# Feed-forward stages in plain record order, and squares kept apart for the ones product

## The chip, the cores and the metric

One core of a Trainium2 chip runs the whole program in one launch. The time is the device time of one execution in microseconds; three executions of the kernel before are shown, and one more was profiled. All data are fp32. TensorE (PE) multiplies, VectorE (DVE) and ScalarE (ACT) work elementwise out of and into on-chip memory, GpSimd (POOL) takes a few additions, and SyncE (SP) issues the loads.

## The reference

512 tokens of width 1024 go through a two-layer transformer and then through one more block. A layer is: half a feed-forward (`swiglu_ffn`), a mixer (banded attentions or recurrences), a cross-attention to a memory, and half a feed-forward again, each behind an RMS norm and added to its input. The last block is a recurrence with sparse attention, an RMS norm, and a feed-forward whose output is normed. Five feed-forwards in all, of width 2816. What the change touches is this:

```python
def rms_norm(x, g):
    y = x * lax.rsqrt(jnp.mean(x * x, axis=-1, keepdims=True) + RMS_EPS)
    return y * g

def swiglu_ffn(x, w_gu, w_down):
    gate, up = jnp.split(x @ w_gu, 2, axis=-1)
    return (jax.nn.silu(gate) * up) @ w_down
```

## The kernel before

The tokens' features lie on the partitions: eight blocks `X[b]` of 128 features by 512 tokens. A product in fp32 is made of three in a shorter type (`mm3`, lines 299 to 305): each factor is split into a high and a low part, hi·hi, hi·lo and lo·hi. Weights are loaded by SP (L296), their high part is cast on ACT (L297) and the low part subtracted on DVE (L298). The inputs of a norm's products are GH (L569, ACT) and GL (L570, DVE), the block times the norm's gain, split; the norm's factor, one per token, is multiplied onto the product's result.

The sum of squares that this factor needs is gathered block by block: ACT squares a block (L166), POOL adds it to `sqacc` (L168). Then a product with a column of ones (L534, in `rms_tokens`; eight matmul records for 512 tokens) sums over partitions, and four transposes (L547) spread the factor over them.

A feed-forward is a list of steps. Two plain groups of 48 matmuls of 512 columns (`plain(0)`, `plain(1)`, each two matrices over eight blocks kt) come first; the ones product is recorded behind the first, `rms.R` behind the second. In the last feed-forward `halves` stands in place of both, with the ones product behind it. Then come units (`unit`): seven products of 24 matmuls of 256 columns on sums and differences of quarters of weights, in place of eight products. Their weights are quarter tiles `fq` (six buffers) summed on DVE (L433, L437, L440, L444) and split on ACT (L416) and DVE (L417), four buffers each; `keep` copies a product's bank aside (L467, ACT), `out` adds it to another bank (L659, L661, DVE), and `act` makes the gate: Silu (L623, ACT), product (L624, DVE), split (L506 ACT, L507 DVE). Among the units stand the steps of the down product (`down`), whose result `add_half` adds to X (L755) and, for the last chunk, hands to `block_done`: GH, GL, square, and for a norm ahead of a feed-forward the sums of two blocks that the units need (`pair_done`, L387 to L392, split by L506 and L507).

The order is made by the tile scheduler: each recorded instruction has its place in the record as its priority, and on each engine the first of those that are ready goes first. `high_priority()` gives what is recorded in it the first place of all; with an offset it shifts the place by so many records. `run_steps` records the preparations (loads and splits) of a step three steps ahead, under `high_priority`. Weights (L296 to L298), GH and GL, the copies of `keep` and the additions of L659 have it too.

Below, A to E are the five feed-forwards in order of time: A 0 to 398 us, B from 831, C from 1184, D from 1999, E from 2887 to the end. Four of them (A, B, C, D) add to X by `add_half`, and each is followed by a mixer or by another stage that starts from X.

Of the kernel before, what the change touches and what calls it, by code (L numbers as in the profile page):

```python
# [18 lines left out]
S = 512  # L19
# [7 lines left out]
NEG = -1e30  # L27
WB = 4

ORDER = (0, 4, 1, 5, 2, 6, 3, 7)  # L30
# [124 lines left out]
class Squares:  # L155
# [4 lines left out]

    def add(self, x):
        first = not self.parts
        if first:
            self.parts.append(self.net.tp.tile([P, 512], F32, name=self.net.uid("sqacc"), tag="sqacc", bufs=1)[:, :])
        sq = self.parts[0] if first else self.net.scratch()
        self.net.nc.scalar.activation(sq, x, AF.Square)  # L166
        if not first:
            self.net.nc.gpsimd.tensor_add(self.parts[0], self.parts[0], sq)  # L168


class Net:
    def __init__(self, ctx, tc, a):
        self.ctx, self.tc, self.nc, self.a = ctx, tc, tc.nc, a
        pool = lambda name, bufs, **k: ctx.enter_context(tc.tile_pool(name=name, bufs=bufs, **k))
        self.cp = pool("const", 1)
        self.wp = pool("weights", 1)
        self.tp = pool("temps", 2)
        self.sp = pool("small", 4)
        self.ps = pool("psum", 8, space=bass.MemoryType.PSUM)
        self.room = ctx.enter_context(tc.tile_pool(name="slots", bufs=38, reuse_waits="tile"))  # L180
        self.live = self.peak = 0
        self.n = 0
        self.scope = None
        self.phase("mix")
        self.setup()
# [34 lines left out]
    def bank(self):  # L220
        t = self.ps.tile([P, 512], F32, name=self.uid("bank"), tag="bank")
        return t

    def small(self, n, tag, bufs=2):
# [62 lines left out]
    def weights(self, w, nk, c):  # L287

        nc = self.nc
        n = nk * c  # L290
        raw = self.wp.tile([P, 1024], F32, name=self.uid("raw"), tag="raw", bufs=2)
        hi = self.wp.tile([P, 1024], F32R, name=self.uid("whi"), tag="whi", bufs=WB)
        lo = self.wp.tile([P, 1024], F32R, name=self.uid("wlo"), tag="wlo", bufs=WB)
        v = lambda t: t[:, :n].rearrange("p (k c) -> p k c", k=nk)
        with self.tc.high_priority():
            nc.sync.dma_start(raw[:, :n], w.block(nk, c))  # L296
            nc.scalar.copy(hi[:, :n], raw[:, :n])  # L297
            nc.vector.tensor_sub(lo[:, :n], raw[:, :n], hi[:, :n].bitcast(F32))  # L298
        return v(hi), v(lo)
# [49 lines left out]

    def feat_group(self, W, order=None):  # L350

        ps = [self.bank() for _ in W]
        order = order or ORDER
        for kt in order:
            for (wh, wl), p in zip(W, ps):
                self.mm3(p, wh[:, kt, :], wl[:, kt, :], self.GH[kt], self.GL[kt], kt == order[0], kt == order[-1])
        return ps
# [62 lines left out]
    def unit(self, load, B, done):  # L420
# [42 lines left out]
        def keep(b, name):  # L463
            def go():
                s = kept[name] = self.get()
                with self.tc.high_priority():
                    nc.scalar.copy(s.f, banks[b])  # L467
            return go
# [19 lines left out]
    def run_steps(self, steps, ahead=3):  # L488

        n = 0  # L490
        for i, (_, go) in enumerate(steps):
            while n < min(len(steps), i + 1 + ahead):
                if steps[n][0]:
                    with self.tc.high_priority():
                        steps[n][0]()
                n += 1
            go()


# [62 lines left out]

    def block_done(self, b, c=slice(0, S)):

        nc = self.nc
        gname, layer = self.gain
        g = self.col(gname, layer * ND + b)
        with self.tc.high_priority():
            nc.scalar.mul(self.GH[b][:, c], self.X[b][:, c], g)  # L569
            nc.vector.scalar_tensor_tensor(self.GL[b][:, c], self.X[b][:, c], g, self.GH[b][:, c].bitcast(F32), OP.mult, OP.subtract)  # L570
        if c.stop == S:
            self.sq.add(self.X[b])
            self.there.add(b)
            if self.pairs is not None and (b + 4) % ND in self.there:
                self.pair_done(b % 4)
# [35 lines left out]
    def ffn(self, nxt, wg, wu, wd, resid, tail=None, also=None):  # L611
# [9 lines left out]
        def act(f, t):  # L621
            g, u = t[:, 0, :], t[:, 1, :]
            nc.scalar.activation(g, g, AF.Silu)  # L623
            nc.vector.tensor_mul(u, u, g)  # L624
            hh, hl = self.get(2)
            self.split(hh.r, hl.r, u)
            HH[f], HL[f] = hh, hl
# [7 lines left out]
        def up(f):  # L635
# [11 lines left out]
            def done(which, bank, slot):  # L647
# [6 lines left out]
                if which == "21":  # L654
                    nc.vector.tensor_mul(o, v(bank), R(c))
                    act(f + 1, T[1])
                    return
                with self.tc.high_priority():
                    nc.vector.tensor_add(o, v(bank), v(slot))  # L659
                if which == "12":  # L660
# [34 lines left out]
        def plain(z):  # L695
            p.extend(self.feat_group(W[z], range(ND) if first else None))
            if z == 0:
                rms.y
            else:
                start()  # L700
# [926 lines left out]
    def out_norm(self, w, XH, XL, gname):  # L1627
# [30 lines left out]
        def update(z, R):  # L1658
            c = half[z]
            for b in ORDER:  # L1660
                m = mix[b].f[:, c]
                (nc.gpsimd if b % 2 else nc.vector).tensor_mul(m, m, R)
                nc.vector.scalar_tensor_tensor(self.X[b][:, c], m, self.col(gname, b), self.X[b][:, c], OP.mult, OP.add)  # L1663
                self.block_done(b, c)

# [364 lines left out]
```

## Time and profile before

| | us |
|---|---|
| three executions | 3302.57, 3307.66, 3314.03 |
| their median | 3307.66 |
| the profiled execution | 3308.28 |
| its span on the core | 3306.5 |
| TensorE busy in it | 3185.9 (96%) |
| VectorE busy | 2254.3 (68%) |
| ScalarE busy | 1609.7 (49%) |
| GpSimd busy | 392.8 (12%) |

The rows below are of the profiled execution. Times in a timeline count from the start of the span. A busy time of two overlapping matmuls counts once. "[12.89 <-POOL sqacc L168]" behind a row means that the engine had stood idle for 12.89 us and that an instruction of POOL on line 168 released it. PEclk 1.00 is the full TensorE clock of 2.4 GHz, 0.50 is 1.2 GHz.

### The profile page before, as it was taken

The numbers are of one execution on the slowest core, as the hardware profiler recorded it, in microseconds if no ns is written. First come the engines' busy times: TensorE is split into PE (matmuls) and PEld (weight loads), VectorE is DVE, ScalarE is ACT, GpSimd is POOL, SyncE is SP. The second block draws the span as 40 slices with busy tenths as digits, with TensorE's granted clock in tenths as the row PEclk, the third lists the DMA queues.
The fourth block names the chain that finished last, engine by engine and source line by source line (L and its number), as shares of the span: only waits on it lengthen the run. The fifth ranks groups of instructions, "written<-read, shape, count | busy, mean of one in ns | idle before, by whom it ended". The sixth has DMA issues, their size and how long they took to land. (4 is left out here: it accounts for less than half of the span.)

```text
span 3306.5 us, 51122 instructions
## 1 busy us (share of the span) xinstructions
PE 3185.9 (96%) x20508; PEld 2864.2 (87%) x20508; DVE 2254.3 (68%) x3384; ACT 1609.7 (49%) x2684; POOL 392.8 (12%) x606
## 2 busy tenths in 40 slices
PE   6999999999999989999999999999999999979998
PEld 5999888898899979998998988999877888769987
DVE  7877656656777688775566557776679455477765
ACT  4544445555444354444455554443486266344434
POOL 1000122201000010001122010000322132220001
PEclk8999998999999999999999999999999999989999
DMA  3333211332233223322223322332322322413331
GB/s 121 116 104 94 82 52 55 106 109 83 79 98 106 90 86 106 104 90 82 90 74 107 120 78 74 106 102 74 103 64 93 106 65 71 153 39 103 102 90 64
DMA packets 104334, 300.81 MB, mean 91 GB/s; under 512 B 13856, under 2 KB 17440, under 8 KB 104096
## 3 DMA queue, kind: packets, MB, share of 16 engines
q1 hardware_dynamic: 94464, 287.74, 27.1%
q10 hardware_dynamic: 9632, 9.80, 1.1%
q8 instruction: 160, 2.62, 0.3%
q14 instruction: 78, 0.64, 0.1%
HBM read 291.21 MB, written 6.29 MB: 90 GB/s over the span
## 5 line engine op out<-in xcount | busy, mean ns | idle before, releaser
L303 PE MATMUL bank<-slot,whi 128*128 128x256 f32 (+1 forms) x2768 | 913.8, 331 | 20.3 <-ACT slot L467 12.2
L304 PE MATMUL bank<-slot,whi 128*128 128x256 f32 (+1 forms) x2768 | 912.2, 330 | 0.2 <-DVE slot L507 0.2
L305 PE MATMUL bank<-slot,wlo 128*128 128x256 f32 (+1 forms) x2768 | 911.8, 330 | 0.0
L416 ACT CAST whi<-fq 128x1024 fp32r<-128x1024 f32 x350 | 365.9, 1048 | 550.3 <-PE bank L304 470.0
L297 ACT CAST whi<-raw 128x1024 fp32r<-128x1024 f32 (+3 forms) x363 | 345.5, 953 | 509.0 <-PE bank L304 286.1
L303 PEld LDWEIGHTS bank<-slot,whi 128*128 128x128 f32 x2768 | 522.6, 189 | 77.8 <-ACT slot L467 16.4
L304 PEld LDWEIGHTS bank<-slot,whi 128*128 128x128 f32 x2768 | 523.0, 189 | 54.5 <-DVE slot L507 3.3
L305 PEld LDWEIGHTS bank<-slot,wlo 128*128 128x128 f32 x2768 | 524.3, 189 | 50.8
L303 PE MATMUL bank<-gh,whi 128*128 128x256 f32 (+1 forms) x1712 | 542.9, 318 | 26.1 <-ACT whi L416 9.2
L298 DVE TENSOR_TENSOR wlo<-raw,whi 128x1024 fp32r<-128x1024 f32 (+3 forms) x363 | 406.7, 1121 | 219.7 <-ACT whi L297 218.3
L304 PE MATMUL bank<-gl,whi 128*128 128x256 f32 (+1 forms) x1712 | 540.6, 316 | 10.1 <-DVE gl L570 9.8
L417 DVE TENSOR_TENSOR wlo<-fq,whi 128x1024 fp32r<-128x1024 f32 x350 | 427.3, 1223 | 174.9 <-ACT whi L416 174.5
L305 PE MATMUL bank<-gh,wlo 128*128 128x256 f32 (+1 forms) x1712 | 538.1, 314 | 0.8 <-DVE wlo L417 0.8
L303 PEld LDWEIGHTS bank<-gh,whi 128*128 128x128 f32 x1712 | 328.0, 192 | 54.8 <-ACT whi L416 11.0
L304 PEld LDWEIGHTS bank<-gl,whi 128*128 128x128 f32 x1712 | 329.2, 192 | 36.9 <-DVE gl L570 14.9
L305 PEld LDWEIGHTS bank<-gh,wlo 128*128 128x128 f32 x1712 | 328.6, 192 | 23.0 <-DVE wlo L417 1.0
L779 PE MATMUL bank<-whi,gh 128*128 128x256 f32 (+1 forms) x1056 | 301.7, 286 | 0.0
L781 PE MATMUL bank<-whi,gl 128*128 128x256 f32 (+1 forms) x1056 | 298.7, 283 | 1.7 <-DVE gl L570 1.7
L780 PE MATMUL bank<-wlo,gh 128*128 128x256 f32 (+1 forms) x1056 | 298.7, 283 | 1.0 <-DVE wlo L298 0.9
L168 POOL TENSOR_TENSOR sqacc<-sqacc,slot 128x512 f32<-128x512 f32 x75 | 118.5, 1580 | 956.7 <-ACT slot L166 916.2
L781 PEld LDWEIGHTS bank<-whi,gl 128*128 128x128 f32 x1056 | 199.8, 189 | 2.2 <-DVE gl L570 2.2
L779 PEld LDWEIGHTS bank<-whi,gh 128*128 128x128 f32 x1056 | 199.7, 189 | 2.1 <-DVE slot L846 0.3
(320 smaller groups left out, 4722.9 us busy)
## 6 DMA issues: line engine op xcount, KB each, us to landing
fq<-in_ffn_w_gu_dram SPq DMA_DIRECT2D x160, 512.0 KB, 3.3
raw<-in_ffn_w_down_dram SPq DMA_DIRECT2D x96, 384.0 KB, 3.1
raw<-in_w_in_dram SPq DMA_DIRECT2D x46, 512.0 KB, 3.4
raw<-in_xa_w_kv_dram SPq DMA_DIRECT2D x32, 512.0 KB, 4.0
raw<-in_od_w_in_dram SPq DMA_DIRECT2D x24, 512.0 KB, 4.0
raw<-in_w_ffn_down_dram SPq DMA_DIRECT2D x22, 512.0 KB, 3.5
fq<-in_w_ffn_gate_dram SPq DMA_DIRECT2D x40, 256.0 KB, 2.7
fq<-in_w_ffn_up_dram SPq DMA_DIRECT2D x40, 256.0 KB, 3.0
```

The source lines that it names most:

```text
L168: self.net.nc.gpsimd.tensor_add(self.parts[0], self.parts[0], sq)
L297: nc.scalar.copy(hi[:, :n], raw[:, :n])
L298: nc.vector.tensor_sub(lo[:, :n], raw[:, :n], hi[:, :n].bitcast(F32))
L303: mm(ps, wh, xh, start=start, stop=False, **k)
L304: mm(ps, wh, xl, start=False, stop=False, **k)
L305: mm(ps, wl, xh, start=False, stop=stop, **k)
L416: self.nc.scalar.copy(hi[:, :n], t[:, :n])
L417: self.nc.vector.tensor_sub(lo[:, :n], t[:, :n], hi[:, :n].bitcast(F32))
L779: mm(o, XH[k][:, t], wh, start=first, stop=False, skip_group_check=True)
L780: mm(o, XH[k][:, t], wl, start=False, stop=False, skip_group_check=True)
L781: mm(o, XL[k][:, t], wh, start=False, stop=last, skip_group_check=True)
```

## The change

While `run_steps` records (`listed`), `first_of_all` gives no priority: preparations, weights, GH and GL of a stage's last blocks, the copies of `keep` and the additions of L659 have the place of their record. Loads recorded outside it (`load_plain` of the first group, those of `halves`, the mixers' weights) keep the first place. The gate's four instructions get a place sixty records later. The ones product of stages A to D is recorded inside the second plain group, before block kt=5: after three blocks in the order 0, 4, 1, 5, ..., and in A, where the blocks go from 0 to 7, after five. The square of the last block of a norm (of the last four for E's norm, `out_norm`'s update) is not added by POOL; it is a part of its own, for which `rms_tokens` records the ones product again.

```diff
@@ -1,5 +1,5 @@
 import math
-from contextlib import ExitStack
+from contextlib import ExitStack, nullcontext
 
 import numpy as np
 
@@ -26,6 +26,8 @@
 EPS = 1e-6
 NEG = -1e30
 WB = 4
+
+LATER = 60
 
 ORDER = (0, 4, 1, 5, 2, 6, 3, 7)
 
@@ -158,13 +160,15 @@
     def __init__(self, net):
         self.net, self.parts = net, []
 
-    def add(self, x):
+    def add(self, x, apart=False):
         first = not self.parts
         if first:
             self.parts.append(self.net.tp.tile([P, 512], F32, name=self.net.uid("sqacc"), tag="sqacc", bufs=1)[:, :])
         sq = self.parts[0] if first else self.net.scratch()
         self.net.nc.scalar.activation(sq, x, AF.Square)
-        if not first:
+        if apart:
+            self.parts.append(sq)
+        elif not first:
             self.net.nc.gpsimd.tensor_add(self.parts[0], self.parts[0], sq)
 
 
@@ -179,6 +183,7 @@
         self.ps = pool("psum", 8, space=bass.MemoryType.PSUM)
         self.room = ctx.enter_context(tc.tile_pool(name="slots", bufs=38, reuse_waits="tile"))
         self.live = self.peak = 0
+        self.listed = False
         self.n = 0
         self.scope = None
         self.phase("mix")
@@ -220,6 +225,10 @@
     def bank(self):
         t = self.ps.tile([P, 512], F32, name=self.uid("bank"), tag="bank")
         return t
+
+    def first_of_all(self):
+
+        return nullcontext() if self.listed else self.tc.high_priority()
 
     def small(self, n, tag, bufs=2):
         t = self.sp.tile([P, n], F32, name=self.uid(tag), tag=tag, bufs=bufs)
@@ -292,7 +301,7 @@
         hi = self.wp.tile([P, 1024], F32R, name=self.uid("whi"), tag="whi", bufs=WB)
         lo = self.wp.tile([P, 1024], F32R, name=self.uid("wlo"), tag="wlo", bufs=WB)
         v = lambda t: t[:, :n].rearrange("p (k c) -> p k c", k=nk)
-        with self.tc.high_priority():
+        with self.first_of_all():
             nc.sync.dma_start(raw[:, :n], w.block(nk, c))
             nc.scalar.copy(hi[:, :n], raw[:, :n])
             nc.vector.tensor_sub(lo[:, :n], raw[:, :n], hi[:, :n].bitcast(F32))
@@ -347,11 +356,13 @@
         v = lambda t: t.rearrange("p (k c) -> p k c", k=ND)
         return [(v(h), v(l)) for h, l in zip(hi, lo)]
 
-    def feat_group(self, W, order=None):
+    def feat_group(self, W, order=None, at=None, also=None):
 
         ps = [self.bank() for _ in W]
         order = order or ORDER
         for kt in order:
+            if kt == at:
+                also()
             for (wh, wl), p in zip(W, ps):
                 self.mm3(p, wh[:, kt, :], wl[:, kt, :], self.GH[kt], self.GL[kt], kt == order[0], kt == order[-1])
         return ps
@@ -463,8 +474,7 @@
         def keep(b, name):
             def go():
                 s = kept[name] = self.get()
-                with self.tc.high_priority():
-                    nc.scalar.copy(s.f, banks[b])
+                nc.scalar.copy(s.f, banks[b])
             return go
 
         def out(which, b, name=None):
@@ -488,13 +498,14 @@
     def run_steps(self, steps, ahead=3):
 
         n = 0
+        self.listed = True
         for i, (_, go) in enumerate(steps):
             while n < min(len(steps), i + 1 + ahead):
                 if steps[n][0]:
-                    with self.tc.high_priority():
-                        steps[n][0]()
+                    steps[n][0]()
                 n += 1
             go()
+        self.listed = False
 
 
     def split(self, hi, lo, src, eng=None):
@@ -560,17 +571,17 @@
         self.pairs = {} if "ffn" in gname else None
         self.there = set()
 
-    def block_done(self, b, c=slice(0, S)):
+    def block_done(self, b, c=slice(0, S), apart=1):
 
         nc = self.nc
         gname, layer = self.gain
         g = self.col(gname, layer * ND + b)
-        with self.tc.high_priority():
+        with self.first_of_all():
             nc.scalar.mul(self.GH[b][:, c], self.X[b][:, c], g)
             nc.vector.scalar_tensor_tensor(self.GL[b][:, c], self.X[b][:, c], g, self.GH[b][:, c].bitcast(F32), OP.mult, OP.subtract)
         if c.stop == S:
-            self.sq.add(self.X[b])
             self.there.add(b)
+            self.sq.add(self.X[b], len(self.there) > ND - apart)
             if self.pairs is not None and (b + 4) % ND in self.there:
                 self.pair_done(b % 4)
 
@@ -620,10 +631,11 @@
 
         def act(f, t):
             g, u = t[:, 0, :], t[:, 1, :]
-            nc.scalar.activation(g, g, AF.Silu)
-            nc.vector.tensor_mul(u, u, g)
-            hh, hl = self.get(2)
-            self.split(hh.r, hl.r, u)
+            with self.tc.high_priority(offset=-LATER):
+                nc.scalar.activation(g, g, AF.Silu)
+                nc.vector.tensor_mul(u, u, g)
+                hh, hl = self.get(2)
+                self.split(hh.r, hl.r, u)
             HH[f], HL[f] = hh, hl
 
         def act_plain(f, pg, pu):
@@ -655,8 +667,7 @@
                     nc.vector.tensor_mul(o, v(bank), R(c))
                     act(f + 1, T[1])
                     return
-                with self.tc.high_priority():
-                    nc.vector.tensor_add(o, v(bank), v(slot))
+                nc.vector.tensor_add(o, v(bank), v(slot))
                 if which == "12":
                     nc.vector.tensor_mul(T[0], T[0], R(slice(0, S)))
                     act(f, T[0])
@@ -693,10 +704,8 @@
                 W.append([self.weights(w, ND, P) for w in ws[2 * z:2 * z + 2]])
 
         def plain(z):
-            p.extend(self.feat_group(W[z], range(ND) if first else None))
-            if z == 0:
-                rms.y
-            else:
+            p.extend(self.feat_group(W[z], range(ND) if first else None, 5 if z else None, lambda: rms.y))
+            if z:
                 start()
 
         def halves():
@@ -1661,7 +1670,7 @@
                 m = mix[b].f[:, c]
                 (nc.gpsimd if b % 2 else nc.vector).tensor_mul(m, m, R)
                 nc.vector.scalar_tensor_tensor(self.X[b][:, c], m, self.col(gname, b), self.X[b][:, c], OP.mult, OP.add)
-                self.block_done(b, c)
+                self.block_done(b, c, 4)
 
         self.table()
         y0, y1 = [], []
```

## Rows read from the trace of the kernel before

**Rows 1.** The page: busy time, share of the span, instructions of each engine.

```profile
PE 3185.9 (96%) x20508; PEld 2864.2 (87%) x20508; DVE 2254.3 (68%) x3384; ACT 1609.7 (49%) x2684; POOL 392.8 (12%) x606
```

**Rows 2.** Stretches: length, then busy PE, PEld, DVE, ACT, POOL (instructions), clock, DMA, GB/s.

```profile
44.40:50.50 6.10, 6.06 (x18) 5.18 (x19) 3.19 (x11) 1.60 (x4) 0.00 (x0) 0.50 0.00 0
...
1197.30:1203.00 5.70, 0.37 (x2) 0.00 (x0) 4.84 (x5) 5.28 (x7) 3.44 (x2) 0.81 0.00 0
...
1203.00:1207.60 4.60, 4.53 (x15) 3.95 (x16) 3.72 (x10) 0.83 (x3) 0.01 (x1) 0.50 0.00 0
...
2942.00:2950.80 8.80, 0.14 (x2) 0.00 (x0) 6.36 (x8) 4.18 (x6) 4.43 (x2) 0.67 0.40 117
...
2950.80:2958.50 7.70, 7.63 (x35) 7.63 (x36) 2.99 (x10) 3.49 (x6) 0.02 (x1) 0.50 0.01 4
...
900.00:1150.00 250.00, 250.00 (x1715) 231.16 (x1714) 188.50 (x208) 105.39 (x133) 0.00 (x0) 1.00 0.30 96
```

**Rows 3.** Waits of PE: what it waited for: total us, times, longest us.

```profile
PE bank L534 <- POOL sqacc L168: 27.0, 3, 12.9
...
PE bank L303 <- ACT slot L467: 12.2, 9, 2.1
...
PE bank L304 <- DVE gl L570: 9.8, 8, 2.3
...
PE bank L303 <- ACT whi L416: 9.2, 9, 1.1
```

**Rows 4.** Timeline of PE, stages A and B: start, duration, engine, line [wait <- releaser].

```profile
44.44 1.86 PE L534 MATMUL bank<-ones,sqacc 128*128 128x1 f32 x8 [12.89 <-POOL sqacc L168]
...
842.32 0.39 PE L305 MATMUL bank<-gh,wlo 128*128 128x512 f32 x1
...
842.55 0.95 PE L534 MATMUL bank<-ones,sqacc 128*128 128x1 f32 x8
...
843.36 0.48 PE L303 MATMUL bank<-gh,whi 128*128 128x512 f32 x1
```

**Rows 5.** Timeline of POOL, ACT and DVE around the wait of stage A.

```profile
43.13 1.26 POOL L168 TENSOR_TENSOR sqacc<-sqacc,slot 128x512 f32<-128x512 f32 x1 [5.19 <-ACT slot L166]
...
42.36 0.62 ACT L166 ACTIVATE slot<-x 128x512 f32<-128x512 f32 x1
...
33.32 1.23 DVE L298 TENSOR_TENSOR wlo<-raw,whi 128x1024 fp32r<-128x1024 f32 x1 [0.25 <-ACT whi L297]
```

**Rows 6.** Timeline of POOL and ACT around the wait of stage E.

```profile
2946.29 4.53 POOL L168 TENSOR_TENSOR sqacc<-sqacc,slot 128x512 f32<-128x512 f32 x2 [8.02 <-ACT slot L166]
...
2943.11 1.99 ACT L416 CAST whi<-fq 128x1024 fp32r<-128x1024 f32 x2 [2.15 <-DVE fq L440]
...
2945.52 1.15 ACT L166 ACTIVATE slot<-x 128x512 f32<-128x512 f32 x2
```

**Rows 7.** Groups by line: count | busy us, mean ns | idle before and its releasers.

```profile
L467 ACT COPY slot<-bank 128x512 f32<-128x512 f32 x150 | 86.0, 581 | 7.0 <-PE bank L1741 6.6 <-issue 0.4
...
L570 DVE SCALAR_TENSOR_TENSOR gl<-x,pv,gh 128x512 fp32r<-128x512 f32 (+1 forms) x88 | 74.4, 859 | 5.0 <-ACT gh L569 4.9
...
L417 DVE TENSOR_TENSOR wlo<-fq,whi 128x1024 fp32r<-128x1024 f32 x350 | 427.3, 1223 | 174.9 <-ACT whi L416 174.5
```

**Rows 8.** Timeline of ACT in the first unit of stage B.

```profile
863.70 1.04 ACT L416 CAST whi<-fq 128x1024 fp32r<-128x1024 f32 x1 [1.21 <-PE bank L304]
...
864.65 0.61 ACT L506 CAST slot<-gu 128x512 fp32r<-128x512 f32 x1
...
865.17 0.58 ACT L467 COPY slot<-bank 128x512 f32<-128x512 f32 x1
```

**Rows 9.** Timeline of DVE and PE where stage A ends.

```profile
394.96 1.72 DVE L298 TENSOR_TENSOR wlo<-raw,whi 128x1024 fp32r<-128x1024 f32 x1
...
396.60 1.77 DVE L570 SCALAR_TENSOR_TENSOR gl<-x,pv,gh 128x512 fp32r<-128x512 f32 x1
...
398.42 0.50 PE L304 MATMUL bank<-gl,whi 128*128 128x512 f32 x1 [0.87 <-DVE gl L570]
```

## The prediction

> **What bounds the kernel now.** I read four views in order. The page's line of busy time says that TensorE works 3185.9 of 3306.5 us, 96% of the span [rows 1]: what a reordering can win lies in the remaining 120.6 us and in matmuls that run at half clock. The table of stretches splits the feed-forward stages. In the 250 us from 900 TensorE is busy for 250.00 us at granted clock 1.00, with DVE at 188.50 (75%) and ACT at 105.39 (42%) [rows 2]: nothing can be won in the middle of a stage, only at its two ends. The list of TensorE's waits then shows which edges matter: three waits of the ones product for POOL's sum of squares, 27.0 us together, 12.9 the longest; and smaller ones for copies of banks (12.2, the longest 2.1), the next norm's inputs GL (9.8) and weight casts (9.2) [rows 3]. Last, the timeline around the largest.
>
> **The ones product, stage by stage.** In stage A the ones product begins at 44.44 after 12.89 us of waiting [rows 4]: TensorE had ended the first plain group at 31.55. The wait ends at POOL's last addition, 43.13 to 44.39, which waited for the square that ACT began at 42.36, queued behind the pair sums' splits [rows 5]. TensorE then restarts at granted clock 0.50, i.e. 1.2 instead of 2.4 GHz, and stays there for the 6.10 us to 50.50 [rows 2]. Stages C and E repeat this: from 1197.30 to 1203.00 TensorE is busy for 0.37 us and from 2942.00 to 2950.80 for 0.14, and each restart runs at 0.50 for 4.60 and 7.70 us [rows 2]. In stage B the squares are ready in time: eight ones matmuls at 842.55, the next product at 843.36, 0.81 us [rows 4]. Stage D is like B.
>
> **What the change does there.** Three edits. The last block's square is no longer added by POOL but is a part of its own, and the ones product takes it directly. In A to D the ones product is recorded inside the second plain group, after three of its eight kt steps (five in A), so 18 or 30 matmuls come ahead of it. And in E's norm the last four squares are apart, so it takes five parts.
>
> Stage A: without the last addition the ones product can begin when the last square ends, 42.36+0.62=42.98. Thirty matmuls are put ahead of it, but the first needs the second plain group's weights. The lo part of the second matrix is made at 33.32 to 34.55 [rows 5], 3 us behind the last matmul of the first group. At 0.23 us each (842.32 to 842.55 [rows 4]) 30 take 6.9 us: from about 34.5 to 41.5. One wait of about 3 us for weights and one of 1.5 us for the square stand where 12.9 stood; 8.4 less, plus part of 6.10×0.5=3 us that the half clock costs, part of which comes back after the 3 us wait. But the records now are plain: the second group's raw load, cast and lo part queue with the first unit's quarter sums in their recorded place, and may come later than 34.5. I take −8; the ends are −4 (weights 4 us later) and −12 (no half clock left).
>
> Stage C: the wait is 5.70−0.37=5.3 us and the half clock costs 4.60×0.5=2.3 [rows 2]. Eighteen matmuls take 4.1 us, so the product asks for the last square at about 1201.4 instead of 1197.3, and the square without POOL's addition, which took 1.26 us in A [rows 5], should be there. I take −6.5, ends −3 and −8.
>
> Stage E: `halves` still asks for the ones product after its features, so nothing is put ahead of it. What goes are POOL's two last additions, 4.53 us from 2946.29; the two squares, on ACT from 2945.52 for 1.15 us, come behind two weight casts of 1.99 us that wait 2.15 us for a quarter sum [rows 6]. If the ACT order stays, the ones product moves from the end of POOL's additions, 2950.82, to 2946.67, 4.2 us; if the preparations, no longer first, let the squares by, the whole wait of 8.80−0.14=8.7 us [rows 2] goes. With it goes up to 7.70×0.5=3.8 us of half clock. Against that, 32 more ones matmuls, 3.2 us by the price below. I take −7: 7 us of the wait, 3.2 of the clock, less 3.2. The ends are −1 and −9.
>
> **The price of parts.** Each extra part is eight matmul records of the ones product, and there are nine norms besides E's that get one, also those ahead of the mixers and cross-attentions, since `block_done` has apart=1 for all. By the row of stage B eight cost 0.81 us, 0.101 each [rows 4]: 9×0.81=+7.3 us, where TensorE is the bound; nothing where it waits anyway. The floor is 0, the ceiling 7.3; I take +7.3, by the row of stage B, where the next product follows at once. The Trainium skill, page "TensorE: Matmul & The Clock Gate", section "Wait — 56ns, not 53.3ns?", says that start to start never falls below about 25 ns however few the columns. By that figure all 104 extra matmuls would be worth an estimated 2.6 us; the row of 0.101 us says four times as much, and I go by the row, which was measured here.
>
> **No first priorities.** Inside a feed-forward stage preparation of weights, copies of banks (150, mean 581 ns) and GH/GL of the next norm (88 GL of 859 ns) [rows 7] lose the first place, and the gates (silu, product, split) are put sixty records behind. Interior: TensorE is saturated, preparation is three steps ahead with four buffers, and DVE has 25% to spare, so 0 as long as that lead holds; if the cover goes, it is rival three. Early units: nine waits each are for a copy and for a cast [rows 3]; the copy stands behind gates. In B the second gate's split runs at 864.65 and the copy only at 865.17, [rows 8], and TensorE waits up to 2.1 us for such copies. Though the copy has first priority it comes behind the split; so what orders it is not priority but, I think, the order in which slots are taken, which is that of the record and which the change leaves. I take 0: ends −24 (these waits, 12.2 and 9.2 us [rows 3], with some half clock behind them) and +8 (gates late, so that a gate buffer is missing).
>
> Ends of the stages: the last GL of a stage runs at 396.60 for 1.77 us behind the mixer's weight part L298 of 1.72 us from 394.96, and TensorE waits 0.87 us for it until 398.42 [rows 9]. Inside the stage GH and GL now are plain while the mixer's weights, recorded outside, are still first: one more L298 ahead of GL is 1.7 us at each of four boundaries. Half of that I take, +3; ends 0 and +8.
>
> Sum: −8 −6.5 −7 +7.3 +0 +3 = −11.2 against the profiled run's 3308.28 us (its span 3306.5), so 3297.1; that run is 0.6 above the median of the three shown, so **3296.5**.
>
> **Rivals.** (1) The early waits go too, because plain gates let the copies by. For it: the ACT in B is idle for 1.21 us ahead of 863.70 [rows 8], so it is order, not load, that keeps the copy. Against it: the copy already had the first priority and stood behind. Of the ends' 24 us about 20: 3276.5. (2) The gains are eaten: the second group's weights come in plain order behind pair sums and quarter sums, so that TensorE waits as long for L298 as it did for POOL, and the boundaries cost more. A −5, C −4, E −3, parts +7.3, boundaries +4 gives −0.7: 3307. (3) Slower: lo parts of the interior (L417, 350 of 1223 ns [rows 7]) come late, since additions out of banks and gates stand ahead of them on DVE in record order. The mechanism decides once the lead of three steps is used up: three products of 24 matmuls at 250.00/1715=0.146 us [rows 2], 10.5 us; DVE at 75% speaks against it, the gate deferral for it. At 1.0 us a unit, the mean of the nine waits for the cast L416 [rows 3], and 350/7=50 units, +50; less the gain of 11: 3347. (4) The change doesn't do what it says: the scheduler orders by readiness, so that removing priorities does nothing; the ones product still gains. That is the forecast itself with boundaries at 0, 3293.5, and is held in it.
>
> **How the numbers follow.** Three runs of before spread over 11 us; 0.3%, 9.9 us, is about what a measurement of this kernel can tell from no change. Chances: forecast 0.46 (own range 3287 to 3306), rival one 0.22, two 0.19, three 0.13. The forecast lies just beyond the bound of 3297.7, so six tenths of it count as faster: 0.46×0.6+0.22 = 0.50 and 0.01 of the second; same 0.18+0.17=0.35; slower 0.13 and 0.01 of the second. The range goes from the far end of rival one, 3272, to past rival two, 3314 (the forecast with parts at full price, boundaries at +8 and the waits shortened by their lower ends, −4 −3 −1 +7.3 +8, is +7.3, 3315); it leaves out rival three.
>
> **What would show it.** Right: no wait of the ones product on POOL, sixteen ones records in the norms of A to D and forty in E; waits of some 3 us for L297/L298 inside the second plain group; no 0.50 clock behind it; the waits for the copies in the early units as before. Wrong: TensorE below 99% between 900 and 1150 (rival three); waits for copies gone (one); a wait for weights of 8 us or more near 32, 1197 or 2942 (two). If sixteen ones matmuls take 1.0 us instead of 1.6, the price of parts was wrong.

## The result and the profile after

The changed kernel took 3275.11 us (median of four runs, 3273.41 to 3276.76), the kernel before 3305.11 (four runs, 3301.63 to 3314.03): ratio 0.9902, 95% interval 0.9887 to 0.9918, or 30 us less. Its profiled execution took 3273.41 us with a span of 3271.6, 34.9 us less than that of before. Line numbers from here on are those of the changed kernel: 2 to 12 higher than before in the parts spoken of (L545 is the ones product, L168 and L172 the square and POOL's addition, L581 GL, L477 the copy of `keep`, L427 the cast of a unit's weights).

The page's line of busy time:

```profile
PE 3179.1 (97%) x20612; PEld 2863.6 (88%) x20612; DVE 2245.2 (69%) x3384; ACT 1611.8 (49%) x2687; POOL 372.0 (11%) x593
```

TensorE's idle time is 3271.6−3179.1 = 92.5 us, where it was 120.6 [rows 1]: 28.1 of the 34.9 us. The other 6.8 are busy time, although 104 matmul records were added; what made the rest cheaper shows in the clock. This is the view of the cores, its mean granted clock last:

```profile
core 0: 3271.6 us, clock 0.988
```

Before it was 0.982. A mean of 0.988 with only the levels 1.00 and 0.50 means that 2.4% of the span, 79 us, ran at half clock; 0.982 means 3.6%, 119 us. So 40 us less of half clock, worth at most 20 us. Another profiled execution of the changed kernel, the run `c_changed_again` below, has a mean of 0.987 and TensorE busy for 3183.8 us: so one kernel shows differences of some 5 us in TensorE's busy time, and a like share of half clock, from execution to execution.

TensorE's waits, as in [rows 3]:

```profile
PE bank L312 <- ACT slot L477: 11.3, 9, 2.1
...
PE bank L312 <- ACT whi L427: 8.0, 8, 1.1
...
PE bank L558 <- DVE nry L537: 6.0, 2, 4.4
...
PE bank L313 <- DVE gl L581: 2.8, 3, 2.3
PE bank L545 <- POOL sqacc L172: 2.8, 1, 2.8
```

The wait of the ones product for POOL fell from 27.0 to 2.8; those for GL at L313 fell from 9.8 to 2.8. The early waits of the units for copies (12.2 to 11.3) and casts (9.2 to 8.0) hardly moved. New is a wait of the transposes (L558) for the norm's root, whose small DVE operations (L537) stand among splits: 1.5 us in stage A, 4.4 in E.

The timeline of TensorE in stage A, then in C and E (compare [rows 4]):

```profile
28.08 0.50 PE L312 MATMUL bank<-gh,whi 128*128 128x512 f32 x1 [0.19 <-ACT whi L306]
...
30.14 0.50 PE L314 MATMUL bank<-gh,wlo 128*128 128x512 f32 x1 [1.32 <-DVE wlo L307]
...
36.29 0.95 PE L545 MATMUL bank<-ones,sqacc 128*128 128x1 f32 x8
37.10 0.48 PE L312 MATMUL bank<-gh,whi 128*128 128x512 f32 x1
...
37.89 0.95 PE L545 MATMUL bank<-ones,slot 128*128 128x1 f32 x8
...
43.98 0.65 PE L558 MATMUL bank<-ident,nry 128*128 128x128 f32 x4 [1.53 <-DVE nry L537]
...
1176.92 0.95 PE L545 MATMUL bank<-ones,sqacc 128*128 128x1 f32 x8
1177.73 1.03 PE L545 MATMUL bank<-ones,slot 128*128 128x1 f32 x8
1178.63 0.48 PE L312 MATMUL bank<-gh,whi 128*128 128x512 f32 x1
...
2899.57 1.86 PE L545 MATMUL bank<-ones,sqacc 128*128 128x1 f32 x8 [2.75 <-POOL sqacc L172]
```

In A nothing waits at the ones product; the two parts are not even side by side, since each goes when its sum or square is there. In C sixteen records take 1.71 us without a wait. In E the sum over the first four squares still waits 2.75 us for POOL.

Where the 34.9 us went, by the starts of the transposes (L547 before, L558 after), which every stage has once its ones product is done:

| stretch | before | after | difference |
|---|---|---|---|
| start to the transposes of A | 59.4 | 44.0 | −15.4 |
| A's units, first mixer, cross-attention, to those of B | 795.2 | 790.1 | −5.1 |
| B's units to those of C | 362.8 | 351.6 | −11.2 |
| C's units, second mixer, cross-attention, D to the last block | 1170.9 | 1174.0 | +3.1 |
| the last block to the transposes of E | 569.6 | 561.6 | −8.0 |
| E's units and the end | 348.6 | 350.3 | +1.7 |

In the other profiled execution of the changed kernel each of these stretches has the same length within 2 us, so the first three and the fifth rows are clear of that spread, and +3.1 and +1.7 hardly are.

### The profile page after: what moved, and what is told of

It is laid out like the page before. It is cut to its first block, busy times and chain, and to the rows that moved or that the text cites. A ratio compares the mean times of both kernels' runs of the same rounds, so it can differ in the third digit from the quotient of the medians.

```text
span 3271.6 us, 51295 instructions
## 1 busy us (share of the span) xinstructions
PE 3179.1 (97%) x20612; PEld 2863.6 (88%) x20612; DVE 2245.2 (69%) x3384; ACT 1611.8 (49%) x2687; POOL 372.0 (11%) x593
## 5 line engine op out<-in xcount | busy, mean ns | idle before, releaser
L312 PE MATMUL bank<-slot,whi 128*128 128x256 f32 (+1 forms) x2768 | 913.0, 331 | 18.5 <-ACT slot L477 11.3
L313 PE MATMUL bank<-slot,whi 128*128 128x256 f32 (+1 forms) x2768 | 910.5, 329 | 0.4 <-DVE slot L518 0.4
L427 ACT CAST whi<-fq 128x1024 fp32r<-128x1024 f32 x350 | 366.5, 1048 | 548.4 <-PE bank L313 461.8
L313 PEld LDWEIGHTS bank<-slot,whi 128*128 128x128 f32 x2768 | 521.5, 188 | 52.2 <-DVE slot L518 1.5
L307 DVE TENSOR_TENSOR wlo<-raw,whi 128x1024 fp32r<-128x1024 f32 (+3 forms) x363 | 407.0, 1122 | 214.5 <-ACT whi L306 213.6
L313 PE MATMUL bank<-gl,whi 128*128 128x256 f32 (+1 forms) x1712 | 537.3, 314 | 2.8 <-DVE gl L581 2.8
L313 PEld LDWEIGHTS bank<-gl,whi 128*128 128x128 f32 x1712 | 326.8, 191 | 26.0 <-DVE gl L581 4.3
L790 PE MATMUL bank<-whi,gl 128*128 128x256 f32 (+1 forms) x1056 | 298.9, 283 | 1.0 <-DVE gl L581 0.8
L172 POOL TENSOR_TENSOR sqacc<-sqacc,slot 128x512 f32<-128x512 f32 x62 | 98.3, 1585 | 924.8 <-ACT slot L168 884.3
L789 PEld LDWEIGHTS bank<-wlo,gh 128*128 128x128 f32 x1056 | 199.9, 189 | 1.8 <-DVE wlo L307 1.6
```

The costliest lines, as they stand in the source:

```text
L312: mm(ps, wh, xh, start=start, stop=False, **k)
L313: mm(ps, wh, xl, start=False, stop=False, **k)
L427: self.nc.scalar.copy(hi[:, :n], t[:, :n])
L789: mm(o, XH[k][:, t], wl, start=False, stop=False, skip_group_check=True)
L790: mm(o, XL[k][:, t], wh, start=False, stop=last, skip_group_check=True)
```

## The experiments

All are timed against the kernel before on the same chip; its medians were 3306.3 to 3307.2 us. Each changes the changed kernel unless it says otherwise. They ran on three chips, and the executions of one kernel spread over 1 to 12 us: a difference of a few us between medians is taken as open where the ranges overlap.

**The ones product behind the first plain group again.**

```diff
-            p.extend(self.feat_group(W[z], range(ND) if first else None, 5 if z else None, lambda: rms.y))
-            if z:
+            p.extend(self.feat_group(W[z], range(ND) if first else None))
+            if z == 0:
+                rms.y
+            else:
                 start()
```

> The changed kernel with the ones product of the first four feed-forwards recorded behind the first plain group again (plain order, later gates and squares apart stay). If the place of the ones product is what removed the waits (theory), TensorE waits again at the end of the first plain group: some 6 us in the first stage, where the last square comes at about 34 us and the group ends at 28, and 3 to 5 us in the third, with half clock behind each: 3275 + 14 = about 3289. If plain order had brought the squares forward so that they are there in any case (rival), there is no wait and the time stays within 3 us of 3275.

3283.69 us, ratio 0.9927 (0.9915 to 0.9939): 9 us slower than the changed kernel. Two waits came back where the theory put them, 5.77 us in A and 1.96 in C, where it had said 3 to 5; that of E, 2.77, is in the changed kernel too. The one in A:

```profile
34.07 1.86 PE L545 MATMUL bank<-ones,sqacc 128*128 128x1 f32 x8 [5.77 <-POOL sqacc L172]
```

That wait is 5.77 us and not 12.89: something else in the change had more than halved it. It is the square kept apart: in the run with plain order and later gates alone, below, which differs from this one only in having every square added, the wait is 12.41 us, the product begins 5.8 us later, and the time is 3.8 us longer, with ranges that overlap. The 14 us expected were too many.

**Every square added by POOL again.**

```diff
-            self.sq.add(self.X[b], len(self.there) > ND - apart)
+            self.sq.add(self.X[b], False)
```

> The changed kernel with every square added by POOL again, one part in every norm. If an extra part costs about 0.81 us of TensorE each time (104 matmul records by 0.1 us, 10.5 us), and the moved ones product leaves POOL time enough in the first four stages, the kernel gets faster there by 7 us and loses about 4 us in the last stage: about 3272. If the parts apart are what lets the ones product go without a wait (rival), waits on POOL of 1 to 5 us come back in three stages: 3280 or more.

3269.30 us, ratio 0.9883 (0.9869 to 0.9897), some 6 us faster than the changed kernel by the medians, with ranges that touch (3265.25 to 3273.89, and 3273.41 to 3276.76). The price of the parts shows in TensorE's busy time, 9.9 us less than with them:

```profile
PE 3169.2 (97%) x20508; PEld 2852.6 (87%) x20508; DVE 2253.3 (69%) x3384; ACT 1611.6 (49%) x2687; POOL 394.7 (12%) x606
```

9.9/104 is 0.095 us a record; the mean clock is 0.989 here, much as there, so it hardly enters, but against the changed kernel's other execution the difference would be 14.6. Waits on POOL are 5.6 us in two: 2.30 in A, which came back, and 3.33 in E, where the changed kernel has 2.75. There is none in B, C or D: there the moved ones product alone is enough. The squares apart do have a use that no one had named. Here is DVE, then TensorE, where C ends in this run, and DVE at the same place of the changed kernel:

```profile
1510.35 1.76 DVE L581 SCALAR_TENSOR_TENSOR gl<-x,pv,gh 128x512 fp32r<-128x512 f32 x1
...
1512.17 0.38 PE L790 MATMUL bank<-whi,gl 128*128 128x256 f32 x1 [1.73 <-DVE gl L581]
```

```profile
1516.42 0.74 DVE L581 SCALAR_TENSOR_TENSOR gl<-x,pv,gh 128x512 fp32r<-128x512 f32 x1
```

With the last square added by POOL (in this run from 1510.31 for 1.26 us) the last GL beside it takes 1.76 us; with the square apart it takes 0.74, and the mixer's wait for it is some 0.9 us shorter. The Trainium skill, page "SBUF — State Buffer", section "Who interferes with whom", says that a DVE instruction with two inputs from that memory contends with a GpSimd instruction that reads it; these two rows agree.

**Plain order and later gates alone**, ones product and squares as in the kernel before (both edits above together).

> The kernel before with plain record order and later gates alone; ones product and squares as before. If the order accounts for little (theory: it is the ones product that pays), within 5 us of the kernel before, 3305. If plain order alone brings the squares and the second group's weights forward in the first stage (rival), the wait of 12.9 us there is halved and the first group ends 3 us earlier: 3305 - 12 = 3293 or less.

3287.45 us, ratio 0.9934 (0.9921 to 0.9947): 20 us under the kernel before. The theory that order accounts for little falls. Of the rival's two reasons the trace shows one:

```profile
39.88 1.86 PE L545 MATMUL bank<-ones,sqacc 128*128 128x1 f32 x8 [12.41 <-POOL sqacc L172]
```

The wait in A is not halved, 12.41 us. But the first group ends at 27.47, 4.1 us earlier than before, and the ones product begins 4.6 us earlier, at 39.88 instead of 44.44.

**Ones product and squares alone**, with first priorities and gates as in the kernel before.

```diff
-        return nullcontext() if self.listed else self.tc.high_priority()
+        return self.tc.high_priority()
...
-                    steps[n][0]()
+                    with self.tc.high_priority():
+                        steps[n][0]()
...
-                nc.scalar.copy(s.f, banks[b])
+                with self.tc.high_priority():
+                    nc.scalar.copy(s.f, banks[b])
...
-                nc.vector.tensor_add(o, v(bank), v(slot))
+                with self.tc.high_priority():
+                    nc.vector.tensor_add(o, v(bank), v(slot))
...
-            with self.tc.high_priority(offset=-LATER):
+            with nullcontext():
```

> The kernel before with the ones product inside the second plain group and the squares apart; first priorities and gates as before. If these edits alone pay (theory), the sum worked out for them holds: -11 in the first stage, -7 in the third, -5 in the last, +7 for the parts: about 3289, and plain order then accounts for the other 14 us. If order does nothing (rival one), 3275. If without plain order the second group's weights come too late (rival two), a wait on the weights of some 8 us takes the place of that on POOL: 3300 or more.

3290.53 us, ratio 0.9946 (0.9933 to 0.9960), 16.7 us under the kernel before, as the theory said. The two halves, 19.8 and 16.7 us, together are 36.5, more than the 30.0 and 31.7 that the whole change brought in its two measurements.

**First priorities again, gates later.** The diff above without its last two lines.

> The changed kernel with all first priorities again (preparations, weights, GH and GL, copies and additions of the units); the gates stay sixty records later, ones product and squares stay changed. If it is the lost first priorities that gave plain order its 16 us (theory), the time goes back to that of the kernel with ones product and squares alone: about 3290. If the later gates gave them (rival), it stays within 4 us of 3275.

3290.70 us, ratio 0.9961 (0.9949 to 0.9974): the theory. What plain order wins is won by taking the first priorities away: 15.6 us, from 3290.70 to 3275.11. In the table's stretches the changed kernel's profiled execution differs from this one by −5.3 (to the transposes of A), +0.1, −6.8 (to C), +3.2, −2.4 (to E) and −4.4 us (the end).

**Only preparations and weights plain**; GH and GL, copies and additions of the units first again.

```diff
-        with self.first_of_all():
+        with self.tc.high_priority():
             nc.scalar.mul(self.GH[b][:, c], self.X[b][:, c], g)
...
-                nc.scalar.copy(s.f, banks[b])
+                with self.tc.high_priority():
+                    nc.scalar.copy(s.f, banks[b])
...
-                nc.vector.tensor_add(o, v(bank), v(slot))
+                with self.tc.high_priority():
+                    nc.vector.tensor_add(o, v(bank), v(slot))
```

> The changed kernel with first priority again for GH and GL, for the copies and for the additions of the units; only preparations and weights stay plain. If it is the preparations, which stood ahead of the last squares and pair sums on ACT and DVE, that matter (theory), the time stays within 4 us of 3275. If first priority of GH and GL or of the units' copies and additions cost the time (rival), about 3285 to 3290.

3272.61 us, ratio 0.9902 (0.9889 to 0.9914), as the changed kernel. So it is the preparations, with the weights that they load and split. Their place shows at the very start, in the queue of SP in the changed kernel:

```profile
1.18 0.42 SPq L332 DMA_DIRECT2D x<-in_x_dram  x1
1.65 0.90 SPq L342 DMA_DIRECT2D raw<-in_ffn_w_gu_dram  x2
2.59 2.40 SPq L332 DMA_DIRECT2D x<-in_x_dram  x4
6.27 0.81 SPq L342 DMA_DIRECT2D raw<-in_ffn_w_gu_dram  x2
7.12 1.38 SPq L332 DMA_DIRECT2D x<-in_x_dram  x3
8.54 2.07 SPq L654 DMA_DIRECT2D fq<-in_ffn_w_gu_dram  x4
```

All eight blocks of X are asked for by 8.07 us, and the quarters of the first unit (L654) after them. Before, the first quarter (then L642) was issued ahead of X, four more among its blocks, and the last three blocks (then L323) came last, the eighth at 13.28 us:

```profile
1.18 0.42 SPq L642 DMA_DIRECT2D fq<-in_ffn_w_gu_dram  x1
...
11.30 2.31 SPq L323 DMA_DIRECT2D x<-in_x_dram  x3
```

This goes with the 5 us of stage A. By what way the preparations cost the other 10 us, most of it where C begins and behind the start of E, was not followed.

**Gates in the place of their record.**

```diff
-            with self.tc.high_priority(offset=-LATER):
+            with nullcontext():
```

> The changed kernel with the gates in the place of their record; all else stays. If the later gates are worth little by themselves (theory: TensorE is busy for 250.00 of 250 us in the middle of a stage with them at either place), within 4 us of 3275. If they are needed in plain order, because a gate now goes ahead of preparations (rival), waits for L427 and L428 appear inside the stages and the time is 3285 or more.

3265.60 us, ratio 0.9883 (0.9870 to 0.9896): faster than the changed kernel by 9.5 us, which neither had said; by the ratios to the kernel before on each chip it is some 6, with intervals that overlap. With the squares apart the later gates cost time. ACT in B's first unit, without them:

```profile
839.79 1.14 ACT L517 CAST slot<-gu 128x512 fp32r<-128x512 f32 x2
841.43 1.04 ACT L427 CAST whi<-fq 128x1024 fp32r<-128x1024 f32 x1 [0.50 <-PE bank L313]
842.38 0.58 ACT L477 COPY slot<-bank 128x512 f32<-128x512 f32 x1
```

and with them, in the changed kernel:

```profile
843.11 1.04 ACT L427 CAST whi<-fq 128x1024 fp32r<-128x1024 f32 x1 [1.02 <-PE bank L313]
844.06 0.61 ACT L517 CAST slot<-gu 128x512 fp32r<-128x512 f32 x1
844.58 0.58 ACT L477 COPY slot<-bank 128x512 f32<-128x512 f32 x1
```

Both splits are done ahead of the cast in the first; in the second one split is left behind the cast, and the copy behind the split. TensorE waits 1.56 instead of 2.08 us for the copy there. The waits for copies fall to 9.7 and for casts to 6.0 us, and the mean clock rises to 0.990. That makes 1.6 and 2.0 us of waits and, as 2.0% instead of 2.4% of the span, some 13 us less of half clock, 6 at most: close to the 9.5, though the clock's part is no larger than the spread between executions of one kernel.

**The first two gates behind the first unit's first product**, every square added by POOL (with the diff of the second experiment as well).

```diff
-            if z:
-                start()
...
-            steps = [(None, lambda: plain(0)), (lambda: load_plain(1), lambda: plain(1))] + up(2)
+            steps = up(2)
+            steps[1:1] = [(None, start)]
+            steps[:0] = [(None, lambda: plain(0)), (lambda: load_plain(1), lambda: plain(1))]
```

> The changed kernel with every square added by POOL again (3269 by its run) and, in the first four feed-forwards, the first two gates recorded behind the first unit's first product, as the last feed-forward has it. If the copy of that product waits for the gates because they are recorded ahead of it (theory), the four waits for the copy of about 2.1 us and the four for the next cast of about 1.2 us go, with some half clock behind them: 3269 - 13 and some = about 3256 to 3261. If the gates are late then themselves (rival), a wait on a split or a bank takes their place: 3269 within 4 us.

3265.28 us, ratio 0.9876 (0.9863 to 0.9889), 4 us under its fellow with all squares added, with ranges that overlap: just outside the rival's 4 us and short of the theory. The waits for copies fell from 10.9 to 5.4 us, as the theory said, but those for casts rose from 8.2 to 10.1.

**Four kernels on one chip**: the changed kernel once more (`c_changed_again`), then three that leave parts of it out.

> The changed kernel itself, to stand beside the next three on one chip: 3275, within 3 us, about 31 us under the kernel before.

3274.63 us (3271.77 to 3276.88), ratio 0.9897 (0.9879 to 0.9914).

Without later gates and squares apart (the diffs of both):

> The changed kernel without its later gates and without the squares apart: plain order and the moved ones product alone. If the gain of 10 us without later gates and the 6 us without the parts are two separate things (theory), about 16 us under the changed kernel: 3259 to 3260. If both are the same thing, or what they gain is the spread between jobs (rival), 3266 or more.

3267.00 us (3265.70 to 3269.49), ratio 0.9875 (0.9860 to 0.9890): 7.6 us under the changed kernel, the rival. The gains of 6 and 9.5 us don't add: with every square added, the gates in place bring 2.3 us (3269.30 to 3267.00), and with the gates in place, adding the squares brings nothing (3265.60 to 3267.00), in both pairs with ranges that overlap. It waits 4.0 us for POOL and 7.2 for GL (4.2 at L313, 3.0 at L790), the changed kernel of the same job 2.8 and 3.8 (2.8 and 1.0).

The last square apart in the norm of A, the last four in that of E, none elsewhere, gates in place:

```diff
-    def block_done(self, b, c=slice(0, S), apart=1):
+    def block_done(self, b, c=slice(0, S), apart=0):
...
             for b in range(4 * z + 1, 4 * z + 4):
-                self.block_done(b)
+                self.block_done(b, apart=1)
...
-            with self.tc.high_priority(offset=-LATER):
+            with nullcontext():
```

> As the one before, but with the last square apart in the first stage's norm and the last four in the last stage's, where the ones product waits for POOL without them (2.7 and 3.6 us in the run with all squares added). If the waits so saved are worth more than 0.8 and 3.2 us of ones products (theory), 2 to 4 us under the one before: about 3256. If in the last stage the 32 matmuls eat the gain (rival), the same as the one before within 2 us.

3264.16 us (3263.42 to 3269.33), ratio 0.9869 (0.9853 to 0.9885): 2.8 us under the one before by the medians, with ranges that overlap. Not decided.

All squares added, gates in place, and the first two gates behind the first product:

> The changed kernel without later gates and squares apart, and with the first two gates of the first four feed-forwards recorded behind the first unit's first product. If the record order decides when that product's copy runs (theory), the four waits of some 2 us for the copy go again: 4 us or more under the run without this edit, about 3255. If the gates in place already took these waits (rival), the same within 2 us.

3262.18 us (3260.95 to 3262.39), ratio 0.9859 (0.9844 to 0.9874): 4.8 us under the same without that edit, with ranges that are apart, and 12.4 under the changed kernel, the fastest here. ACT in B's first unit, where the copy now comes ahead of the gates:

```profile
836.19 0.59 ACT L477 COPY slot<-bank 128x512 f32<-128x512 f32 x1
836.80 1.28 ACT L635 ACT_TABLE_LOAD   x1
838.10 0.63 ACT L635 ACTIVATE gu<-gu 128x512 f32<-128x512 f32 x1
```

The waits for copies fell from 9.3 to 4.2 us. The record order does decide when this copy runs.

## Why the prediction was right in sign, and where its terms were off

It forecast a faster kernel at 3296.5; the range held 3275.1, 21 us under the point. That it held is luck: its lower end was that of the first rival, and the forecast's own range, 3287 to 3306, misses. The time is almost that of this rival, 3276.5, but not by its mechanism: the early waits that it let go are still there (21.4 us of copies and casts before, 19.3 after).

The terms for the ones product and the parts, −8 −6.5 −7 +7.3 = −14.2, were sound as a sum: these edits alone brought 16.7 us. The step that failed is "No first priorities", with the ends of the stages: it took +3, and the first priorities taken away brought −15.6. Point by point:

**Stage A: forecast −8, measured −15.4 with its part's 0.8.** What failed here is "without the last addition the ones product can begin when the last square ends, 42.36+0.62=42.98": it kept the time of that square from the trace of before [rows 5]. The square itself came 6.3 us earlier. ACT in the changed kernel, then in the run with ones product and squares alone, where first priorities hold it at 43.32:

```profile
35.56 0.62 ACT L517 CAST slot<-slot 128x512 fp32r<-128x512 f32 x1 [1.30 <-DVE slot L403]
36.08 0.63 ACT L168 ACTIVATE slot<-x 128x512 f32<-128x512 f32 x1
```

```profile
43.32 0.63 ACT L168 ACTIVATE slot<-x 128x512 f32<-128x512 f32 x1
```

With the ones product moved and first priorities kept, the transposes of A begin at 50.0; with plain order and later gates alone, at 54.7; with all of it, at 44.0: −9.4 and −4.7 give −14.1, nearly all of −15.4. The forecast priced the first of these (−8) and not the second. It asked whether the second group's weights would come later in plain order and let first priorities be free elsewhere; it didn't follow the queue of SP and DVE ahead of the first group, where the first unit's quarters stood before blocks of X and the eighth block was asked for at 13.28 us, not 8.07. The three waits for GL in A's first group, 1.34, 2.11 and 1.28 us before, are gone with it; one of 2.84 us for the weights' low part (L353) is new. The weights in plain order were no trouble: 0.19 and 1.32 us of waiting where the forecast had about 3.

**Stage C: forecast −6.5.** The wait of 5.3 us is gone and the clock is 1.00 behind it. This row of stretches spans its first group's end and its units:

```profile
1176.00:1186.00 10.00, 10.00 (x54) 8.39 (x53) 6.62 (x12) 6.16 (x8) 0.00 (x0) 1.00 0.04 15
```

The stretch from B's transposes to C's lost 11.2 us, in which the waits for GH and GL where B ends have a part, the next point. With ones product and squares alone it lost 6.8, close to the forecast; with plain order and later gates alone 4.4. The order's share, again, had been put at nothing.

**Ends of the stages: forecast +3, and of the wrong sign.** TensorE's waits for GH and GL where B, C and D end, in the kernel before (A's is in [rows 9], 0.87):

```profile
1192.03 0.50 PE L303 MATMUL bank<-gh,whi 128*128 128x512 f32 x1 [0.49 <-ACT gh L569]
1193.13 0.50 PE L304 MATMUL bank<-gl,whi 128*128 128x512 f32 x1 [0.60 <-DVE gl L570]
...
1549.15 0.39 PE L781 MATMUL bank<-whi,gl 128*128 128x256 f32 x1 [0.56 <-DVE gl L570]
...
2356.54 0.42 PE L781 MATMUL bank<-whi,gl 128*128 128x328 f32 x1 [1.16 <-DVE gl L570]
```

The changed kernel has these two at A and C, and none at B and D:

```profile
378.05 0.50 PE L313 MATMUL bank<-gl,whi 128*128 128x512 f32 x1 [0.31 <-DVE gl L581]
...
1517.21 0.38 PE L790 MATMUL bank<-whi,gl 128*128 128x256 f32 x1 [0.80 <-DVE gl L581]
```

3.68 us became 1.11, so the term is −2.6 (most of the fall from 9.8 to 2.8 in the list of waits lies elsewhere, 4.7 of it at the start of A). The argument was that the mixer's L298 would get ahead of a plain GL. At A's end it stands ahead of it as before (L307 at 374.57 for 1.72 us, GL at 376.20), but no more of them do. B's two waits are gone in every run with plain order or with later gates, and stay (0.41 and 0.60 us) with ones product and squares alone. At C and D it is the last GL, which no longer runs beside POOL's addition of the last square: with every square added TensorE waits 1.73 us at C and 1.17 at D.

**Stage E: forecast −7.** From the last block's second transposes the way to E's is 37.1 us, was 41.7: −4.6. This wait before,

```profile
2950.87 1.87 PE L534 MATMUL bank<-ones,sqacc 128*128 128x1 f32 x8 [8.73 <-POOL sqacc L168]
```

became 2.75 us, on POOL, for the four squares that are still added; the transposes now wait 4.4 us for the root. The term lay inside its ends, −9 and −1, but two of its signs failed here: a wait on POOL is left, and the eight records behind it take 1.73 us, at half clock. Nor were the parts needed: the way is 36.1 us with plain order and later gates alone, where one product waits 3.55 us, 37.5 with ones product and squares alone, 36.5 in the changed kernel with every square added. Plain order with later gates was enough here.

**The price of parts: forecast +7.3 and 3.2 in E, confirmed as TensorE's time.** 0.101 us a record was taken from the row of B; the changed kernel's rows have 0.81 us for eight (36.29 to 37.10), and taking all 104 out freed 9.9 us of TensorE, 0.095 each. In the kernel's time it is open what they cost: 5.8 us with later gates, nothing that shows with gates in place.

**Early units: forecast 0, confirmed**, and with the reason given, as far as the record order goes: it holds the copy, as the runs with gates behind the first product show. That it works through the order in which slots are taken, as the prediction thought, no run shows. In the changed kernel the first copy of B is waited for as before:

```profile
845.21 0.39 PE L312 MATMUL bank<-slot,whi 128*128 128x256 f32 x1 [2.08 <-ACT slot L477]
```

**Interior: forecast 0, confirmed**; rival three did not come:

```profile
880.00:1130.00 250.00, 250.00 (x1710) 231.11 (x1709) 186.67 (x206) 104.82 (x134) 0.00 (x0) 1.00 0.31 97
```

**Later gates** had no term of their own; they stood at 0 with the interior. Taking them out brought 9.5 us with the squares apart and 2.3, not clear of the spread, with every square added. Why this and the gain from adding the squares don't sum is not settled. What differs between runs from A's transposes to B's (779.7 us with every square added, 790.1 in the changed kernel) was not followed.

## What to carry to other kernels

A first priority orders everything behind it, loads included: before pricing its removal, list what stands first in each queue at the start and at each change of stage, and move the times of all that follow. Put a small reduction inside a block of matmuls that don't need it rather than between two blocks; then, in three of four stages here, its operands needed no special care, and extra parts for it gained nothing that showed in the time. If a copy waits although it is first in priority, look at what is recorded ahead of it.

## What was not expected of the hardware

Of 34.9 us gained in the profiled runs, busy time of TensorE is 6.8 in spite of some 10 us of added matmuls: about 17 us, by this estimate, come from less time at 1.2 GHz, 119 us before and 79 after (it would be 12 by the changed kernel's other execution). The restarts behind the long waits, at 0.50 for 6.10, 4.60 and 7.70 us [rows 2], were counted; the half clock in other stages was not. From the transposes of A to those of B the mean granted clock rose from 0.98 to 0.99.

The Trainium skill, page "TensorE: Matmul & The Clock Gate", section "Wait — 56ns, not 53.3ns?", has about 25 ns as the least from one matmul's start to the next. The ones product took 0.095 to 0.101 us a record in these runs, so that figure was no guide to it.
